# mLSTM heads: Silu in one activation, and the last two heads' convolutions behind the first head's scores

## The chip, the core and the metric

One Trainium2 chip, one of its cores, one launch. The time is the device time of a launch in microseconds, which here is the time of that core. Five engines work from instruction streams of their own: PE (TensorE, matmuls), DVE (VectorE), ACT (ScalarE), POOL (GpSimd) and SP (SyncE); the last two mostly issue DMAs in this kernel.

## The reference

A decoder layer on 512 tokens of width 1024, in float32: an mLSTM branch with 4 heads and a sliding-window attention branch (SWA) with 16 query heads, 4 key heads and a window of 128 run on the same normalised input, are gated and merged, and an MLP and a gated embedding follow. The part that the change touches makes the queries and keys of the mLSTM branch:

```python
qk_ml = jax.nn.silu(causal_depthwise_conv(qk_ml, conv_qk[i]))      # 4 taps along the tokens
q_ml, k_ml = jnp.split(qk_ml, 2, axis=-1)
q_ml = q_ml.reshape(B, S, ML_HEADS, ML_DQK) * (ML_DQK ** -0.5)     # 4 heads of 128
k_ml = k_ml.reshape(B, S, ML_HEADS, ML_DQK)
...
h_ml = mlstm_chunkwise(q_ml, k_ml, v_ml..., ig, lf)                # scores, decay, num / den
y_b = swa_with_sinks(q_sw, k_sw, v_sw, sinks[i])
```

## The kernel before

A matrix product is made of three passes of a faster float format: each float32 operand is split into a high part (a cast, `split` or `load_w`, on ACT) and a low part (the residual, on DVE), and high x high, low x high and high x low are added up in PSUM. So each weight block costs ACT a cast of 128 x 1024 (`wh`) and DVE a residual (`wl`). In PSUM there are three pools of two tiles each: `psg` for projections, `psa` for scores and transposes, `pst` for the outputs of the attention and the rest. Tiles of 128 x 512 in SBUF (`acc`, `sg`, `dm` and others) come from one ring of 34. Names in the profile are those of the tiles; `qs` is a split query of the attention, `yb` its split output, `lm` a tile of logits and then weights, `ya` the parts that the mLSTM heads use.

In which order an engine gets its instructions is set by a list scheduler that takes them in the order of the code with costs of its own, and lets a later one pass an earlier one on an engine where that one would wait. So the order below isn't the order of the code. ACT evaluates functions from a table; where the next function isn't in the loaded one, an ACT_TABLE_LOAD stands ahead of it. Exponentials, Sigmoid and Silu each ask for a load where another of the three ran before; copies and casts don't.

Two stretches matter:

- The attention loop, 236 to about 325 us: 16 units (`swa_probs`, four query heads on one block of 128 tokens each), whose scores are made two units ahead of the unit at hand. Every four units `swa_out` transposes two blocks' weights and multiplies them with the values. Between the units `fill` puts projections: those of the attention's queries (`q_proj`) and seven of the eight mLSTM tiles (`qk_proj`, in the order 0, 4, 1, 5, 2, 6, 3; tiles 0 to 3 are the heads' queries, 4 to 7 their keys).
- The head stage, about 325 to 390 us: decay matrices (`ml_decay`, exponentials on ACT), the last projection, Silu, the split into parts (`qk_parts`), scores and outputs of the four heads (`ml_scores`, `ml_out`), with blocks of the attention's branch product (`branch_b`) between.

Before, `qk_proj` convolves straight from PSUM: ACT scales the tile by the last tap into `acc`, DVE adds the three shifted taps (L854), and only then is the PSUM tile free. `silu` takes a new tile `sg` for the sigmoid and multiplies on DVE (L862), with the queries' factor 128^-0.5 in the same instruction.

Of the kernel before, what the change touches and what calls it, by code (L numbers as in the profile page):

```python
# [12 lines left out]
AF = mybir.ActivationFunctionType  # L13
ALU = mybir.AluOpType
AX = mybir.AxisListType

P = 128
S = 512
# [5 lines left out]
NH = 4  # L24
# [75 lines left out]
def block_kernel(  # L100
# [32 lines left out]
    V, A, G, T = nc.vector, nc.scalar, nc.gpsimd, nc.tensor  # L133
# [18 lines left out]
    def nm(s):  # L152
        n_names[0] += 1
        return f"{s}_{n_names[0]}"


    def ps_g():
        return pp.tile([P, 512], F32, tag="g", bufs=2, name=nm("psg"))

    def ps_t():  # L160
        return pp.tile([P, 512], F32, tag="t", bufs=2, name=nm("pst"))

    def ps_a():
        return pp.tile([P, 1024], F32, tag="a", bufs=2, name=nm("psa"))
# [6 lines left out]
    def act_f(n="f"):  # L171
        return ap.tile([P, 512], F32, tag="act", bufs=NACT, name=nm(n))
# [21 lines left out]
    def r32(t):  # L194
        return t.bitcast(F32)
# [3 lines left out]
    def split(dst, src, scale=None):  # L199

        if scale is None:
            A.copy(dst[0], src)  # L202
            last_low[0] = V.tensor_sub(dst[1], src, r32(dst[0]))  # L203
        else:
            done = A.activation(dst[0], src, AF.Copy, scale=scale)
            V.scalar_tensor_tensor(dst[1], src, scale, r32(dst[0]), ALU.mult, ALU.subtract)
            return done
# [13 lines left out]
    def load_w(src, n, dims, raw=None, cast=False):  # L221

        if raw is None:
            raw = load_raw(src, n)
        parts = [wp.tile([P, 1024], F32R, tag=t, bufs=WB, name=nm(t))[:, :n] for t in ("wh", "wl")]
        if cast:
            nc.gpsimd.dma_start(out=parts[0], in_=src)
            last_low[0] = V.tensor_sub(parts[1], raw[:, :n], r32(parts[0]))
        else:
            split(parts, raw[:, :n])  # L230
        return [q.rearrange("p (k c) -> p k c", k=dims) for q in parts]

    def pairs(a, b):

        return [(a[0], b[0]), (a[0], b[1]), (a[1], b[0])]
# [19 lines left out]
    def mm_T(ps, w, acts, first=True, last=True):  # L255

        ops = []
        for k in range(len(acts)):
            ops += pairs([q[:, k, :] for q in w], acts[k])
        chain(ps, ops, first, last)  # L260
# [31 lines left out]
    def cols(src, n, name, pool=cp):  # L292
        t = pool.tile([P, n], F32, name=name)
        nc.sync.dma_start(out=t, in_=src)
        return t
# [37 lines left out]
    cw = cols(conv, KT * 4, "cw", c1)  # L333
# [127 lines left out]
    for m in range(NT):  # L461
# [7 lines left out]
        ps = ps_g()  # L469
# [7 lines left out]
    def proj_T(wd, i, bank=ps_g):  # L477
        ps = bank()
        mm_T(ps, load_w(wd[i], KT * P, KT), hT)
        return ps  # L480
# [49 lines left out]
    for i in range(2):  # L530
        ps = ps_t()
# [3 lines left out]
        for ab in range(2):  # L535
            s, o = HALF[ab], HALF[1 - ab]
# [309 lines left out]

    qk = [None] * 8

    def qk_proj(i):
        ps = proj_T(w_qkml, i)  # L850
        acc = act_f("acc")
        A.activation(acc, ps, AF.Copy, scale=cw[:, i * 4 + 3 : i * 4 + 4])
        for s in range(1, 4):
            V.scalar_tensor_tensor(  # L854
                acc[:, s:], ps[:, : S - s], cw[:, i * 4 + 3 - s : i * 4 + 4 - s], acc[:, s:], ALU.mult, ALU.add
            )
        qk[i] = acc

    def silu(i):
        sg = act_f("sg")  # L860
        A.activation(sg, qk[i], AF.Sigmoid)
        V.scalar_tensor_tensor(qk[i], qk[i], P**-0.5 if i < 4 else 1.0, sg, ALU.mult, ALU.mult)  # L862


    yb = [None] * 8
# [108 lines left out]
    def spare():  # L974

        k = turn[0] % KT
        turn[0] += 1
        return [t[:, k, :] for t in ya_parts]

    def qk_parts(h):  # L980
        for i in (h, 4 + h):
            hl = spare()
            split(hl, qk[i])
            qk[i] = hl

    hs = [[act_f("hs") for _ in range(2)] for _ in range(NH)]
# [7 lines left out]
    def ml_decay(h):  # L994
        pr = rows[h]
        dg = act_f("dg")
        V.tensor_tensor(
            dg.rearrange("p (t j) -> p t j", t=NT),
            pr.rearrange("p (t j) -> p t j", t=NT),
            tri.unsqueeze(1).broadcast_to([P, NT, P]),  # L1000
            ALU.add,
        )
        dm = [act_f("dm") for _ in range(3)]
        wT = [dm[0], dm[1][:, :384], dm[2][:, :256], dm[2][:, 256:384]]
        for s in range(NT):
            for t in range(s, NT):
                src = dg if t == s else pr
                A.activation(
                    wT[s][:, (t - s) * P : (t - s + 1) * P],
                    src[:, t * P : (t + 1) * P],  # L1010
                    AF.Exp,
                    bias=gc[:, t * NT + s, h : h + 1],
                )
        wts[h] = dm, wT

    def ml_scores(h):

        two, one = ps_a(), ps_t()
        psc = [two[:, :512], two[:, 512:896], one[:, :256], one[:, 256:]]
        q, k = qk[h], qk[4 + h]  # L1020
        for s in range(NT):
            n0 = min(s, 2) * P
            ops = pairs([t[:, s * P : (s + 1) * P] for t in k], [t[:, n0:] for t in q])
            for j, (l, r) in enumerate(ops):
                T.matmul(psc[s], l, r, start=j == 0, stop=j == 2, skip_group_check=True)
        dm, wT = wts[h]
        hl = []
        for j, n in enumerate((512, 384, 384)):
            for s in ((0,), (1,), (2, 3))[j]:
                V.tensor_mul(wT[s], psc[s][:, P:] if s == 3 else psc[s], wT[s])  # L1030
            hl.append([t[:, :n] for t in spare()])
            split(hl[j], dm[j][:, :n])
        wts[h] = hl + [[t[:, 256:] for t in hl[2]]]
# [40 lines left out]
    def branch_b(i):  # L1074
        ps = ps_g()
        mm_T(ps, load_w(w_b[i], KT * P, KT, cast=True), yb)
        t2[i] = act_f("gb")
        V.tensor_mul(t2[i], ps, gate_of(gbd, i))
# [9 lines left out]

    ml_decay(0)
    qk_proj(7)  # L1090
    silu(0)
    silu(4)
    qk_parts(0)
    ml_scores(0)
    for h in range(1, NH):
        silu(h)
        silu(4 + h)
    rds = []
    todo = list(range(KT))
    for h in range(NH):  # L1100
        for _ in range(1 if h else 2):
            branch_b(todo.pop(0))
        if h + 1 < NH:
            ml_decay(h + 1)
            qk_parts(h + 1)
        with tc.issue_after(last_mm[0].ins):
            rds.append(ml_out(h))
        if h + 1 < NH:
            if h == 2:
                branch_b(todo.pop(0))  # L1110
            with tc.issue_after(last_mm[0].ins):
                ml_scores(h + 1)
        if h == 1:
            ml_norm([0, 1], rds)
        elif h > 1:
            ml_norm([h], rds[h:])
# [703 lines left out]
    def one(n):  # L1820
        return tp.tile([P, 1], F32, tag=n, bufs=4, name=nm(n))
# [49 lines left out]
    for m in range(NT):  # L1871
        for o, n in ((0, 512),) if m == 0 else ((0, 256), (256, 256)):
            ps = ps_g()[:, :n]
# [4 lines left out]
            if o == 0:  # L1878
                s = one("fse")
# [115 lines left out]
```

## Time and profile before

| | |
|---|---|
| runs | 863.28, 864.51, 865.06 us; median 864.51 |
| the profiled execution's own time | 864.57 us |
| its span in the profile | 862.7 us |
| granted clock of PE | 0.998 |
| busy: PE, weight load, DVE, ACT, POOL | 851.6, 741.1, 724.1, 530.4, 61.2 us |
| DMA | 125.7 MB, mean 146 GB/s |

The page's times are those of one execution. Busy time of an engine is the union of its instructions; a matmul's end is modelled, so the pace of PE is better read from the starts of its matmuls. A bracket behind a row of the timeline is the idle time of that engine ahead of the row and the instruction that ended it. A group's row gives its count, its busy time and the mean of one, then the idle time ahead of the group.

### The profile page before, as it was taken

The page shows a single profiled execution, that of the slowest core. Times are in us where ns is not written, and L with a number is a line of the kernel's source. Part 1 is how long each engine was busy: PE and PEld are TensorE (multiplying, and loading weights), DVE is VectorE, ACT ScalarE, POOL GpSimd, SP SyncE. Part 2 cuts the span into 40 slices and gives each one's busy share as a digit, 9 for nine tenths or more (in the row PEclk, how much of TensorE's full clock was granted, in tenths as well). Part 3 has the DMA queues.
Part 4 walks back from the last instruction along what each step waited for, and adds up shares of the span by engine and source line. Part 5 has one row for each costly group of instructions (what it writes and reads, how often), then busy time and mean ns, then how long its engine had stood idle before and what let it go on. Part 6 is the DMA issues. An engine that isn't in the chain of part 4 may idle for free.

```text
span 862.7 us, 12945 instructions
## 1 busy us (share of the span) xinstructions
PE 851.6 (99%) x4926; PEld 741.1 (86%) x4926; DVE 724.1 (84%) x1059; ACT 530.4 (61%) x913; POOL 61.2 (7%) x93
## 2 busy tenths in 40 slices
PE   9999999999999999999999999999999999999996
PEld 7888789999878777888888888899889989988886
DVE  7898879777788888867897799879988997899656
ACT  6776657555587667864343586458638744774743
POOL 3121111000000000000020000000000000010000
PEclk9999999999999999999999999999999999999999
DMA  8677235444411246565324381744365364634402
GB/s 289 204 179 295 89 144 189 155 147 146 148 49 50 98 147 226 202 252 200 122 39 133 98 234 38 221 129 137 75 193 147 104 174 133 172 104 131 138 1 97
DMA packets 37967, 125.70 MB, mean 146 GB/s; under 512 B 5261, under 2 KB 5261, under 8 KB 37906
## 3 DMA queue, kind: packets, MB, share of 16 engines
q1 hardware_dynamic: 28578, 95.77, 32.6%
q0 software_dynamic: 9184, 28.85, 13.9%
q8 instruction: 38, 0.62, 0.3%
q10 hardware_dynamic: 144, 0.26, 0.1%
q14 instruction: 23, 0.19, 0.1%
HBM read 106.51 MB, written 11.54 MB: 137 GB/s over the span
## 4 chain that ended last, share of the span: by engine, by line
PE 86%; issue 5%; DVE 4%; ACT 2%; DMA 2%; SPq 0%; POOL 0%; POOLq 0%; DVEq 0%; ACTq 0%
PE psp L1382 27%; PE psg L241 24%; PE psa L241 11%; PE psg L1382 9%; PE psp L241 6%; PE pst L241 4%; ACT lm L900 1%; DMA wr<-in_w_vsif 1%; PE psp L1213 1%; PE pst L945 1%; PE psa L875 1%; PE psa L876 1%; PE psa L911 1%; DVE wl L203 0%; DMA wh<-in_w_b 0%
## 5 line engine op out<-in xcount | busy, mean ns | idle before, releaser
L202 ACT CAST wh<-wr 128x1024 fp32r<-128x1024 f32 x90 | 94.8, 1054 | 81.1 <-PE psg L241 20.9
L203 DVE TENSOR_TENSOR wl<-wr,wh 128x1024 fp32r<-128x1024 f32 x90 | 109.5, 1220 | 35.7 <-ACT wh L202 35.3
L1382 PE MATMUL psp<-x,wh 128*128 128x256 f32 x672 | 121.3, 283 | 0.0
L1382 PE MATMUL psp<-wh,uf 128*128 128x512 f32 x336 | 106.1, 390 | 0.1
L1382 PEld LDWEIGHTS psp<-x,wh 128*128 128x128 f32 x672 | 105.0, 192 | 0.3
L1367 ACT CAST wh<-wr 128x1024 fp32r<-128x1024 f32 x59 | 60.5, 1049 | 59.7 <-DVE wr L1707 26.4
L1382 PE MATMUL psp<-x,wl 128*128 128x256 f32 x336 | 95.1, 283 | 0.0
L1370 DVE TENSOR_TENSOR wl<-wr,wh 128x1024 fp32r<-128x1024 f32 x59 | 71.2, 1219 | 10.3 <-ACT wh L1367 8.0
L1382 PEld LDWEIGHTS psp<-wh,uf 128*128 128x128 f32 x336 | 63.1, 188 | 14.3 <-issue 1.3
L1367 ACT CAST wh<-wd 128x1024 fp32r<-128x1024 f32 x45 | 47.2, 1049 | 33.0 <-PE psp L1382 27.8
L1382 PE MATMUL psp<-wl,uf 128*128 128x512 f32 x168 | 65.5, 390 | 0.0
L1382 PEld LDWEIGHTS psp<-x,wl 128*128 128x128 f32 x336 | 64.5, 192 | 0.0
L241 PE MATMUL psg<-h,wh 128*128 128x512 f32 x192 | 60.9, 395 | 0.7 <-DVE acc L854 0.7
L1370 DVE TENSOR_TENSOR wl<-wd,wh 128x1024 fp32r<-128x1024 f32 x45 | 54.7, 1218 | 3.1 <-ACT wh L1367 3.1
L241 PEld LDWEIGHTS psg<-h,wh 128*128 128x128 f32 x192 | 35.1, 188 | 7.5 <-DVE acc L854 0.9
L1400 DVE TENSOR_TENSOR uf<-F,uf 128x512 fp32r<-128x512 f32 (+3 forms) x36 | 35.0, 983 | 6.4 <-ACT uf L1399 6.4
L241 PE MATMUL psg<-yb,wh 128*128 128x512 f32 x128 | 40.0, 392 | 0.0
L241 PE MATMUL psg<-h,wl 128*128 128x512 f32 x96 | 37.7, 393 | 0.0
L1382 PEld LDWEIGHTS psp<-wl,uf 128*128 128x128 f32 x168 | 31.5, 188 | 6.7 <-DVE wl L1370 0.3
L1382 PE MATMUL psg<-wh,uf 128*128 128x512 f32 x112 | 36.5, 389 | 0.0
L1399 ACT CAST uf<-F 128x512 fp32r<-128x512 f32 (+3 forms) x36 | 30.7, 857 | 7.6 <-DVE F L1417 7.1
L241 PE MATMUL psg<-ya,wh 128*128 128x512 f32 x112 | 34.9, 391 | 0.0
(409 smaller groups left out, 2221.6 us busy)
## 6 DMA issues: line engine op xcount, KB each, us to landing
wr<-in_w_down SPq DMA_DIRECT2D x16, 512.0 KB, 4.6
wd<-in_w_down SPq DMA_DIRECT2D x16, 512.0 KB, 4.4
wr<-in_w_upb SPq DMA_DIRECT2D x12, 512.0 KB, 4.2
wd<-in_w_upb SPq DMA_DIRECT2D x12, 512.0 KB, 4.5
gd<-gr POOLq DMA_DIRECT2D x8, 512.0 KB, 2.9
wr<-in_w_qkml SPq DMA_DIRECT2D x8, 512.0 KB, 3.4
wr<-in_w_b SPq DMA_DIRECT2D x8, 512.0 KB, 3.4
wh<-in_w_b POOLq DMA_DIRECT2D x8, 512.0 KB, 4.6
```

The lines of the kernel that those rows point to most:

```text
L202: A.copy(dst[0], src)
L203: last_low[0] = V.tensor_sub(dst[1], src, r32(dst[0]))
L241: last_mm[0] = T.matmul(ps, l, r, start=first and i == 0, stop=last and i == len(ops) - 1, skip_group_check=parts)
L875: T.matmul(o, q[:, n * P : (n + 1) * P], kk[kp][ab][:, k0 : k0 + 256], start=True, stop=False)
L876: T.matmul(o, q[:, n * P : (n + 1) * P], kl[kp][ab][:, k0 : k0 + 256], start=False, stop=True)
L900: A.activation(lm3[:, g, :], lm3[:, g, :], AF.Exp, bias=nmx[:, g : g + 1], scale=0.125, accum_out=sm[:, g : g + 1])
L911: T.transpose(pt[:, c : c + P], pT[:, c : c + P], ident)
L1367: return [A.copy(parts[0], slots[user])]
L1370: return [V.tensor_sub(parts[1], slots[user], r32(parts[0]))]
L1382: yield T.matmul(ps, l, r, start=first and j == 0, stop=last and j == len(ops) - 1, skip_group_check=True)
L1399: h = sca(n / 512 * 0.48 + 0.05, lambda: A.copy(dst()[0], src()), deps)
L1400: return vec(n / 512 * 0.54 + 0.06, lambda: V.tensor_sub(dst()[1], src(), r32(dst()[0])), [h])
```

## The change

The convolution becomes a function of its own. Tiles of heads 0 and 1 are convolved from PSUM as before; those of heads 2 and 3 are copied from PSUM by ACT, and convolved from the copy behind the first head's scores. Sigmoid and product become one Silu in place, and the queries' factor goes into the scale of the split. The Silus of heads 0 and 1 are written ahead of the first scores, those of heads 2 and 3 behind the first head's outputs.

```diff
--- before.py
+++ after.py
@@ -846,20 +846,25 @@
 
     qk = [None] * 8
 
+    def convolve(i, src):
+        acc = act_f("acc")
+        A.activation(acc, src, AF.Copy, scale=cw[:, i * 4 + 3 : i * 4 + 4])
+        for s in range(1, 4):
+            V.scalar_tensor_tensor(
+                acc[:, s:], src[:, : S - s], cw[:, i * 4 + 3 - s : i * 4 + 4 - s], acc[:, s:], ALU.mult, ALU.add
+            )
+        qk[i] = acc
+
     def qk_proj(i):
         ps = proj_T(w_qkml, i)
-        acc = act_f("acc")
-        A.activation(acc, ps, AF.Copy, scale=cw[:, i * 4 + 3 : i * 4 + 4])
-        for s in range(1, 4):
-            V.scalar_tensor_tensor(
-                acc[:, s:], ps[:, : S - s], cw[:, i * 4 + 3 - s : i * 4 + 4 - s], acc[:, s:], ALU.mult, ALU.add
-            )
-        qk[i] = acc
+        if i % 4 < 2:
+            convolve(i, ps)
+        else:
+            qk[i] = act_f("qk")
+            A.copy(qk[i], ps)
 
     def silu(i):
-        sg = act_f("sg")
-        A.activation(sg, qk[i], AF.Sigmoid)
-        V.scalar_tensor_tensor(qk[i], qk[i], P**-0.5 if i < 4 else 1.0, sg, ALU.mult, ALU.mult)
+        A.activation(qk[i], qk[i], AF.Silu)
 
 
     yb = [None] * 8
@@ -980,7 +985,7 @@
     def qk_parts(h):
         for i in (h, 4 + h):
             hl = spare()
-            split(hl, qk[i])
+            split(hl, qk[i], P**-0.5 if i < 4 else None)
             qk[i] = hl
 
     hs = [[act_f("hs") for _ in range(2)] for _ in range(NH)]
@@ -1088,13 +1093,12 @@
 
     ml_decay(0)
     qk_proj(7)
-    silu(0)
-    silu(4)
+    for i in (0, 4, 1, 5):
+        silu(i)
     qk_parts(0)
     ml_scores(0)
-    for h in range(1, NH):
-        silu(h)
-        silu(4 + h)
+    for i in (2, 6, 3, 7):
+        convolve(i, qk[i])
     rds = []
     todo = list(range(KT))
     for h in range(NH):
@@ -1110,6 +1114,9 @@
                 branch_b(todo.pop(0))
             with tc.issue_after(last_mm[0].ins):
                 ml_scores(h + 1)
+        if h == 0:
+            for i in (2, 6, 3, 7):
+                silu(i)
         if h == 1:
             ml_norm([0, 1], rds)
         elif h > 1:
```

Where the change puts the activations: the first place is ACT in the attention loop, around 246 us, behind the copy of unit 5's logits (`lm_441`). In the kernel before, the exponentials of unit 3 (`lm_415`) follow:

```order
L888 COPY lm_441_2695<-psa_448_2715 128x512
L900 ACTIVATE lm_415_2565,sm_432_2640<-lm_415_2565,nmx_429_2634 128x128 x2
L897 ACTIVATE es_431_2638<-ds_430_2636 128x4
L900 ACTIVATE lm_415_2565,sm_432_2640<-lm_415_2565,nmx_429_2634 128x128 x2
L553 CAST qs_439_2683<-psg_434_2649 64x512
L912 COPY lm_400_2510<-psa_455_2743 128x1024
```

In the changed kernel (its line numbers are five higher here):

```order
L893 COPY lm_441_2695<-psa_448_2715 128x512
L867 ACT_TABLE_LOAD
L867 ACTIVATE acc_426_2616<-acc_426_2616 128x512
L902 ACT_TABLE_LOAD
L902 ACTIVATE es_431_2638<-ds_430_2636 128x4
L905 ACTIVATE lm_415_2565,sm_432_2640<-lm_415_2565,nmx_429_2634 128x128 x4
L553 CAST qs_439_2683<-psg_434_2649 64x512
L902 ACTIVATE es_445_2704<-ds_444_2702 128x4
```

The Silu of tile 0 (`acc_426`) has come up to here, with a table load ahead of it and another one ahead of the exponentials; three more Silus stand in the loop like this, and ACT has 24 table loads in the program, against 14.

The second place is PE some 20 us later: scores of unit 8 (`psa_495`, four pairs that need the queries 391, 438, 472 and 486), then a projection (`psg_503`) and the scores of unit 9 (`psa_508`). Before, the four pairs of unit 8 stand together, and the projection follows whole:

```order
L875 MATMUL psa_495_2928<-kk_98_541,qs_438_2680 128x256
L876 MATMUL psa_495_2928<-kl_100_543,qs_438_2680 128x256
L875 MATMUL psa_495_2928<-kk_98_541,qs_472_2828 128x256
L876 MATMUL psa_495_2928<-kl_100_543,qs_472_2828 128x256
L875 MATMUL psa_495_2928<-kk_98_541,qs_486_2894 128x256
L876 MATMUL psa_495_2928<-kl_100_543,qs_486_2894 128x256
L241 MATMUL psg_503_2956<-h_31_197,wh_505_2959 128x512
L241 MATMUL psg_503_2956<-h_32_198,wh_505_2959 128x512
L241 MATMUL psg_503_2956<-h_31_197,wl_506_2960 128x512
```

Now unit 9's first pairs and the projection's first matmuls have come between the third pair and the fourth:

```order
L880 MATMUL psa_495_2928<-kk_98_541,qs_472_2828 128x256
L881 MATMUL psa_495_2928<-kl_100_543,qs_472_2828 128x256
L880 MATMUL psa_508_2992<-kk_99_542,qs_392_2417 128x256
L881 MATMUL psa_508_2992<-kl_101_544,qs_392_2417 128x256
L880 MATMUL psa_508_2992<-kk_99_542,qs_439_2683 128x256
L881 MATMUL psa_508_2992<-kl_101_544,qs_439_2683 128x256
L241 MATMUL psg_503_2956<-h_31_197,wh_505_2959 128x512
L241 MATMUL psg_503_2956<-h_32_198,wh_505_2959 128x512
L241 MATMUL psg_503_2956<-h_31_197,wl_506_2960 128x512
L880 MATMUL psa_495_2928<-kk_98_541,qs_486_2894 128x256
L881 MATMUL psa_495_2928<-kl_100_543,qs_486_2894 128x256
```

The number of matmuls ahead of the third pair is the same in both.

The third place is what feeds PE there, DVE. Before, the residuals of the queries (`qs`, which free the projections' PSUM tiles 468 and 482) stand right behind the last residual of the attention's outputs (`yb`):

```order
L203 TENSOR_TENSOR yb_467_2786<-pst_459_2770,yb_466_2785 128x128
L203 TENSOR_TENSOR yb_467_2786<-pst_458_2765,yb_466_2785 128x128
L554 TENSOR_TENSOR qs_472_2828<-psg_468_2797,qs_472_2828 64x512
L554 TENSOR_TENSOR qs_473_2831<-psg_468_2797,qs_473_2831 64x512
L901 TENSOR_TENSOR sm_480_2854<-sm_480_2854,es_479_2852 128x4
L903 RECIPROCAL rc_481_2860<-sm_480_2854 128x4
L554 TENSOR_TENSOR qs_486_2894<-psg_482_2863,qs_486_2894 64x512
```

Now the residual of a weight block (`wl_557`) and a mask copy (L894) stand ahead of the second of them:

```order
L203 TENSOR_TENSOR yb_467_2786<-pst_459_2770,yb_466_2785 128x128
L908 RECIPROCAL rc_481_2860<-sm_480_2854 128x4
L909 TENSOR_TENSOR lm_475_2843<-lm_475_2843,rc_481_2860 128x512
L203 TENSOR_TENSOR yb_467_2786<-pst_458_2765,yb_466_2785 128x128
L203 TENSOR_TENSOR wl_557_3231<-wr_555_3228,wh_556_3230 128x1024
L554 TENSOR_TENSOR qs_472_2828<-psg_468_2797,qs_472_2828 64x512
L894 COPY_PREDICATED lm_475_2843<-later_key_92,psa_488_2900 128x512
L554 TENSOR_TENSOR qs_473_2831<-psg_468_2797,qs_473_2831 64x512
L554 TENSOR_TENSOR qs_486_2894<-psg_482_2863,qs_486_2894 64x512
```

On ACT the cast of that weight block (`wh_556`) has likewise moved from behind the third of these queries to ahead of the last output cast. The fourth place is DVE where unit 14's logits (`lm_580`) are reduced. Before, the residual ahead of it is `wl_642`, the reduction of unit 14 follows two rows later:

```order
L889 COPY_PREDICATED lm_580_3354<-later_key_92,psa_579_3345 128x512
L228 TENSOR_TENSOR wl_642_3643<-wr_640_3640,wh_641_3642 128x1024
L901 TENSOR_TENSOR sm_564_3282<-sm_564_3282,es_563_3280 128x4
L891 TENSOR_REDUCE mx_581_3357<-lm_580_3354 128x4
L903 RECIPROCAL rc_565_3288<-sm_564_3282 128x4
L893 SCALAR_TENSOR_TENSOR nmx_582_3359<-mx_581_3357,nsink_2494 128x4
```

Now it is `wl_644`, a load later of the branch's weights, and the normalisation of unit 13 and the mask's product (L923) have gone ahead of it:

```order
L906 TENSOR_TENSOR sm_564_3279<-sm_564_3279,es_563_3277 128x4
L908 RECIPROCAL rc_565_3285<-sm_564_3279 128x4
L909 TENSOR_TENSOR lm_547_3207<-lm_547_3207,rc_565_3285 128x512
L923 SCALAR_TENSOR_TENSOR pT_568_3308<-tri_97,psa_567_3298 128x1024
L894 COPY_PREDICATED lm_580_3351<-later_key_92,psa_579_3342 128x512
L228 TENSOR_TENSOR wl_644_3666<-wr_642_3663,wh_643_3665 128x1024
L896 TENSOR_REDUCE mx_581_3354<-lm_580_3351 128x4
L898 SCALAR_TENSOR_TENSOR nmx_582_3356<-mx_581_3354,nsink_2494 128x4
```

## The prediction

> **What bounds the kernel now.** I read the busy shares first, then the chain that ended last, then the busy time by stretches, and last the waits of TensorE (PE) in the stage that the change touches.
>
> ```profile
> PE 851.6 (99%) x4926; PEld 741.1 (86%) x4926; DVE 724.1 (84%) x1059; ACT 530.4 (61%) x913; POOL 61.2 (7%) x93
> ...
> PEclk9999999999999999999999999999999999999999
> ...
> PE 86%; issue 5%; DVE 4%; ACT 2%; DMA 2%; SPq 0%; POOL 0%; POOLq 0%; DVEq 0%; ACTq 0%
> ```
>
> PE is busy for 99% of the span at the full granted clock, and 86% of the chain is PE's. So a change that leaves PE's matmuls as they are can only move the time through PE's gaps: it wins those that it closes and loses those that it opens. The stretches of the stage show how much room the feeding engines have:
>
> ```profile
> core 0: us, PE busy (x) PEld busy (x) DVE busy (x) ACT busy (x) POOL busy (x), PEclk, DMA share, GB/s
> 240.00:260.00 20.00, 18.95 (x100) 14.00 (x99) 18.65 (x42) 16.54 (x54) 0.00 (x0) 1.00 0.19 55
> ...
> 340.00:360.00 20.00, 19.79 (x123) 17.63 (x122) 15.36 (x34) 15.43 (x45) 1.06 (x2) 1.00 0.67 237
> ```
>
> Columns: length, then the busy time of each engine. In 240 to 260 us VectorE (DVE) has 1.35 us free and ScalarE (ACT) 3.46; here are also PE's only early gaps. Its waits over 236 to 400 us:
>
> ```profile
> PE pst L945 <- DVE pT L918: 0.7, 1, 0.7
> PE psg L241 <- DVE acc L854: 0.7, 1, 0.7
> PE psa L875 <- DVE lm L889: 0.2, 1, 0.2
> PE psa L1025 <- DVE hd L1049: 0.2, 1, 0.2
> PE psa L911 <- DVE nmx L893: 0.2, 1, 0.2
> ...
> 250.88 0.63 PE L911 MATMUL psa<-ident,lm 128*128 128x128 f32 x4 [0.15 <-DVE nmx L893]
> ...
> 323.98 1.08 PE L945 MATMUL pst<-pT,vs 128*64 128x512 f32 x4 [0.69 <-DVE pT L918]
> ```
>
> That is 2.0 us in all, each wait for DVE; two of them stand below with their place in the timeline. This is the whole of what the change can win in this stage, a little more if measured from start to start (below).
>
> **The change part by part.** The rows that price it, ACT and then DVE, grouped over 236 to 345 us (busy, mean ns of one, idle before):
>
> ```profile
> L900 ACT ACTIVATE lm<-lm,nmx 128x128 f32<-128x128 f32 x64 | 25.0, 392 | 10.9 <-DVE nmx L893 10.7
> L888 ACT COPY lm<-psa 128x512 f32<-128x512 f32 x11 | 6.4, 584 | 0.3 <-PE psa L876 0.2
> L852 ACT ACTIVATE acc<-psg,cw 128x512 f32<-128x512 f32 x8 | 5.4, 678 | 1.6 <-PE psg L241 1.6
> L861 ACT ACTIVATE sg<-acc 128x512 f32<-128x512 f32 x8 | 5.0, 659 | 0.0
> L861 ACT ACT_TABLE_LOAD x1 | 1.3, 1283 | 0.0
> ...
> L203 DVE TENSOR_TENSOR wl<-wr,wh 128x1024 fp32r<-128x1024 f32 x7 | 8.5, 1212 | 0.0
> L854 DVE SCALAR_TENSOR_TENSOR acc<-psg,cw,acc 128x511 f32<-128x511 f32 x8 | 5.9, 741 | 0.3 <-ACT acc L852 0.3
> L862 DVE SCALAR_TENSOR_TENSOR acc<-acc,sg 128x512 f32<-128x512 f32 x8 | 5.2, 681 | 0.0
> L554 DVE TENSOR_TENSOR qs<-psg,qs 64x512 fp32r<-64x512 f32 x6 | 4.1, 688 | 1.1 <-ACT qs L553 0.8
> ```
>
> - Removed: eight products on DVE, 8 x 0.681 = 5.4 us. They stood where PE had only the 0.7 us wait for pT, so most of this was hidden work.
> - Added: four copies of PSUM to a tile on ACT, 4 x 0.584 = 2.3 us. They free PSUM earlier for the tiles of heads 2 and 3, but the one PE wait for the convolution (psg L241 <- acc L854) belongs to tile 0, which is convolved as before. Gain: nothing.
> - Moved: four convolutions go from the attention loop to behind the first head's scores, 4 x 3 x 0.741 = 8.9 us of DVE and 4 x 0.678 = 2.7 us of ACT. DVE has 4.64 us free in 340 to 360 and the product work is gone there, so the cover is the matmuls of the head stage; if it runs short, the next split or decay product comes late to PE. I take 0.3 us, with 0 and 1.5 as ends (a third of the surplus of 8.9 over 4.64).
> - The factor of q goes into the split: the scaled forms cost at most 678 against 662 and 741 against 681 by the nearest rows, four tiles, 0.3 us of hidden work.
> - Silu itself has no row. By Sigmoid (659) and the scaled copy (678) of the same shape its 8 take what the 8 Sigmoids took; if it took two of them, 5.3 us more would lie on ACT, some 0.66 at each site below.
>
> **What really moves is where the activation runs.** Sigmoid wrote a new tile and all eight stood together, behind one table load. The in-place Silu needs no tile, and in the changed order of ACT four of them stand singly inside the attention loop, each with a load ahead of it and one for the exponentials behind it: ten more loads in the program, eight in the loop, 10 x 1.283 = 12.8 us of ACT. Where a load falls now shows its price:
>
> ```profile
> 245.79 0.59 ACT L888 COPY lm<-psa 128x512 f32<-128x512 f32 x1
> 246.41 0.40 ACT L900 ACTIVATE lm<-lm,nmx 128x128 f32<-128x128 f32 x1
> ...
> 257.58 0.27 ACT L202 CAST yb<-pst 128x128 fp32r<-128x128 f32 x1 [1.02 <-PE pst L945]
> ...
> 260.81 0.42 ACT L202 CAST yb<-pst 128x128 fp32r<-128x128 f32 x2
> ...
> 305.79 0.27 ACT L202 CAST yb<-pst 128x128 fp32r<-128x128 f32 x1 [1.49 <-PE pst L945]
> ...
> 309.01 0.47 ACT L202 CAST yb<-pst 128x128 fp32r<-128x128 f32 x2 [0.19 <-DVE yb L203]
> ...
> 322.88 0.69 ACT L852 ACTIVATE acc<-psg,cw 128x512 f32<-128x512 f32 x1 [1.57 <-PE psg L241]
> 323.59 1.28 ACT L861 ACT_TABLE_LOAD   x1
> 324.88 0.63 ACT L861 ACTIVATE sg<-acc 128x512 f32<-128x512 f32 x1
> ```
>
> The load at 323.59 starts 0.02 us after the activation before it and is followed 0.01 us later by the Sigmoid: it costs its own 1.28 and nothing around it. A pair with its Silu is 1.28 + 0.66 + 1.28 = 3.2 us that ACT cannot give to the exponentials.
>
> [...]
>
> **Site 1, at 246.4.** Before, unit 3's exponentials follow the copy at 245.79; now the pair stands between. The exponentials of units 3 to 5 shift 3.2 us, and the order lets PE run 15 other matmuls ahead of the block's outputs (pst). PE's pace is read here:
>
> ```profile
> 255.59 1.08 PE L945 MATMUL pst<-pT,vd 128*64 128x512 f32 x4
> ...
> 264.89 0.28 PE L875 MATMUL psa<-kk,qs 128*128 128x256 f32 x1
> ...
> 265.42 0.63 PE L241 MATMUL psg<-h,wh 128*128 128x512 f32 x2
> ...
> 270.64 0.39 PE L241 MATMUL psg<-h,wl 128*128 128x512 f32 x1
> ```
>
> The 24 matmuls from 265.42 to 270.64 start 0.228 us apart, so 15 of them are 3.4 us: the outputs start near 259.0 instead of 255.59, PE does not wait at this place, and its wait for nmx goes. The price comes one step on. ACT's eight output casts (yb) began at 257.58 and were done with at 261.2; now they begin at 257.58 + 3.4 = 261.0. Unit 6's four exponentials, which ran partly among the query casts, now stand among them, and a weight cast of 1.05 us stands ahead of the last. The same mixture of eight casts and four exponentials took from 305.79 to 309.48, 3.7 us; with the weight cast the last yb is out at 261.0 + 3.7 + 1.05 = 265.75. DVE then owes the last yb residual (a cast's time, 0.27), the wl of that weight (1.21) and the query residual qs_472 (0.69): 267.9. PE's third pair of unit 8's scores needs that tile, has the same matmuls ahead of it in both orders, and arrived at 264.89, now 0.3 earlier: 264.6. It waits 3.3. Behind it a mask copy (as long as a product, 0.7) and qs_473 (0.69) take DVE to 269.3, which frees the PSUM tile of psg_503; PE, with six score matmuls left (four take 0.53 from 264.89 to 265.42, so 0.8), stands there at 268.7 and waits 0.6 more. Sum 3.9 if every cast of this chain is as late as I say, 2.9 if the 1.02 that ACT was idle ahead of the first cast is made up. I take 3.5; the ends are 0 (the first rival) and 6.4, the pair (3.2) on top of the 3.2 by which ACT is late already.
>
> **Sites 2 and 3**, the pairs around tiles 4 and 1: ACT had idle time there and the projection is fed from copies; what is late next is the first transposes of a block, at about PE's arrival. 0.2 us, ends 0 and 1.3 (a load exposed).
>
> **Site 4**, the pair ahead of units 12 and 13. The rows are DVE's and POOL's of before:
>
> ```profile
> 305.25 0.68 DVE L891 TENSOR_REDUCE mx<-lm 128x4 f32<-128x512 f32 x1
> ...
> 309.51 0.68 DVE L904 TENSOR_TENSOR lm<-lm,rc 128x512 f32<-128x512 f32 x1
> ...
> 309.42 0.54 POOL L227 DMA_DIRECT2D wh<-in_w_b  x1 [11.45 <-DVE rc L903]
> ...
> 314.03 1.23 DVE L228 TENSOR_TENSOR wl<-wr,wh 128x1024 fp32r<-128x1024 f32 x1 [0.39 <-DMA wh<-in_w_b]
> ```
>
> The branch's weights are loaded by POOL when PE has used up a buffer, and a residual on DVE (L228) waits for them: 4.6 us from issue to use for the second load, which gets the buffer of psg_587. Before, only the first load's residual stood ahead of unit 14's reduction, and the second behind unit 15's; in the new order the second stands right ahead of unit 14's. From the end of psg_587's chain it is 0.1 to the issue, 4.6 for the load, 1.2 for the residual, and 4.9 from reduction to normalised weights (305.25 to 310.19): 10.8 us. PE has 28 projection matmuls, 6 outputs, 8 scores and 8 transposes before unit 14's transposes, 34 x 0.228 + 16 x 0.13 = 9.8. It waits 1.0; the pair itself has delayed units 12 and 13, and what of that reaches this chain comes on top. Between 0 (the load is covered) and 3.2 (the pair whole) I take 1.2.
>
> **The sum.** Opened: 3.5 + 0.2 + 1.2 + 0.3 = 5.2 us. Closed: the waits for nmx, pT and hd, 0.2 + 0.7 + 0.2 in the table; from start to start, where the next matmul could have come 0.228 after the last, they are 0.3, 0.8 and 0.4, so 1.5. The waits for lm and acc stand ahead of the first pair and stay. Net +3.7 us. The profiled execution took 864.57 (span 862.7 and 1.87 around it), 0.06 above the median of 864.51: 868.3 against the one, 868.2 against the other.
>
> **The rivals.**
> 1. Hidden: ACT is idle for 39% of the span and the scores run two units ahead, so the pairs fit in ACT's gaps and PE sees none. For it: 10.7 us of idle before exponentials (the L900 row), which are waits for DVE that a later start can overlap. Against: the late casts meet DVE when it has 1.35 us to spare in 20, and PE's order is interleaved with DVE's step by step at 265. Time: 864.5, within 1.
> 2. Faster: with 5.4 us of products gone and 8.9 us of convolutions out of the loop, DVE, the engine in every one of the five waits, is always early. It decides from the point where the four pairs open less than 1 us together and the waits close. Against: two of the five stand before anything has left DVE. At most all 2.7 us (start to start) go: 861.8.
> 3. Every load exposed: the exponentials are on the path each time. The waits at 250.88 and 323.98 show that the softmax chain is close to PE at two places; against it, at the other two ACT works ahead. 10 x 1.283 on top: 877.4.
> [...]
>
> [...]
>
> **How the numbers follow.** Forecast (opened 4 to 7 us, so 867 to 870): 0.53. Hidden: 0.26. Faster: 0.08. Loads exposed: 0.10. Pipe emptied: 0.03. A difference under 0.2%, 1.7 us, cannot be told from none, so faster is 0.08, same 0.26 and slower 0.66. The range leaves out the faster case and most of the last two: 863.4 to 872.5; the likeliest case by itself is 867 to 870.
>
> **What would show it.** Right: eight more ACT_TABLE_LOADs between 246 and 310 us, in pairs around single Silus; a PE wait of 3 to 4 us near 265 to 270, for DVE's qs; one of 1 to 2 us ahead of unit 14's transposes near 320, behind a wl that waited for its load; ACT busier by 12.8 + 2.3 = 15 us, DVE less busy by 5.4; Silu near 660 ns. Wrong: qs cast at 261 to 265 as before (the casts were not pushed), or the four Silus back in one place, or a gap in 340 to 360 behind DVE's convolutions, which would mean that the move costs and not the loads.

## The result, and the profile after

The changed kernel takes 871.18 us (median of six runs, 868.89 to 872.27) against 864.25 us in the same runs before: 1.0078 times as long, 95% interval 1.0064 to 1.0092. The forecast was 868.2 within 863.4 to 872.5; the result lies in this range, and above the likeliest case of 867 to 870. The profiled execution is the longest of the six, 872.27 us, so its gaps show a little more than the median does.

The page's busy times, and PE's waits over 236 to 410 us (engine and line, waited for; us in all, times, longest):

```profile
PE 854.0 (98%) x4926; PEld 741.3 (85%) x4926; DVE 722.2 (83%) x1051; ACT 544.7 (63%) x927; POOL 61.3 (7%) x93
...
PE psa L880 <- DVE qs L554: 2.5, 1, 2.5
PE psa L1091 <- DVE ya L206: 1.9, 1, 1.9
PE psg L241 <- DVE acc L853: 0.7, 1, 0.7
PE psa L916 <- DVE lm L909: 0.6, 1, 0.6
PE psa L880 <- DVE lm L894: 0.5, 2, 0.3
```

ACT is 14.3 us busier and DVE 1.9 us less, with the same matmuls on PE. The old waits for nmx, pT and hd are gone; two long ones have come, for `qs` and for `ya`.

Both programs have 4926 matmuls, so the start of the n-th can be compared. How much later it starts than before:

| matmul | 1000 | 1600 | 1700 | 1800 | 1900 | 2000 | 2100 | 2300 | 2400 | 4900 |
|---|---|---|---|---|---|---|---|---|---|---|
| starts, before (us) | 174.36 | 259.36 | 277.90 | 297.55 | 316.03 | 337.80 | 353.97 | 389.95 | 410.67 | 852.04 |
| later by (us) | 0.53 | 0.23 | 4.22 | 4.23 | 4.40 | 4.69 | 5.12 | 4.43 | 7.82 | 7.76 |

Two steps make the loss: 4.0 us between matmuls 1600 and 1700, and 3.4 us between 2300 and 2400. (The first 0.5 comes ahead of anything that the change touches, and is absent or of the other sign in other traces below.)

**The first step.** ACT at the first load pair, then DVE and PE twenty us later:

```profile
246.31 0.59 ACT L893 COPY lm<-psa 128x512 f32<-128x512 f32 x1
246.92 1.28 ACT L867 ACT_TABLE_LOAD   x1
248.22 0.63 ACT L867 ACTIVATE acc<-acc 128x512 f32<-128x512 f32 x1
248.85 1.28 ACT L902 ACT_TABLE_LOAD   x1
250.15 0.21 ACT L902 ACTIVATE es<-ds 128x4 f32<-128x4 f32 x1
...
266.11 1.22 DVE L203 TENSOR_TENSOR wl<-wr,wh 128x1024 fp32r<-128x1024 f32 x1
267.36 0.69 DVE L554 TENSOR_TENSOR qs<-psg,qs 64x512 fp32r<-64x512 f32 x1
268.07 0.73 DVE L894 COPY_PREDICATED lm<-later_key,psa 128x512 f32<-128x512 int32 x1
268.84 1.41 DVE L554 TENSOR_TENSOR qs<-psg,qs 64x512 fp32r<-64x512 f32 x2
...
268.10 0.38 PE L880 MATMUL psa<-kk,qs 128*128 128x256 f32 x1 [2.49 <-DVE qs L554]
...
269.59 0.73 PE L241 MATMUL psg<-h,wh 128*128 128x512 f32 x2
```

The pair with its Silu takes 3.2 us of ACT, and each load is followed within 0.02 us of its end by the next activation. Then the chain of the forecast runs link by link: the weight residual, the first query residual, and PE's third pair of unit 8's scores the moment that one is done.

**The second step** is 130 us later. SP, DVE and PE around the last head's normalisation, then PE's clock in two stretches (columns as before; granted clock third from the end):

```profile
387.18 0.33 SPq L1176 DMA_DIRECT2D wo<-in_w_out  x1
...
393.28 1.22 DVE L1187 TENSOR_TENSOR wo<-wo,wo 128x1024 f32<-128x1024 f32 x1 [4.58 <-DMA wo<-in_w_out]
394.42 0.17 DVE L391 RECIPROCAL rs<-sd 128x4 f32<-128x4 f32 x1
...
399.14 0.66 PE L1091 MATMUL psa<-ident,hs 128*128 128x128 f32 x4 [1.88 <-DVE ya L206]
...
400.87 1.05 PE L241 MATMUL psg<-yb,wh 128*128 128x512 f32 x2
401.72 0.63 PE L241 MATMUL psg<-yb,wl 128*128 128x512 f32 x1
...
396.77:400.18 3.41, 1.53 (x10) 1.03 (x9) 3.41 (x5) 0.35 (x1) 0.00 (x0) 1.00 0.82 303
400.18:403.60 3.42, 3.42 (x10) 2.53 (x9) 1.91 (x3) 0.70 (x2) 0.00 (x0) 0.50 0.53 194
```

DVE in the kernel before:

```profile
387.23 0.18 DVE L391 RECIPROCAL rs<-sd 128x4 f32<-128x4 f32 x1 [2.96 <-ACT sd L389]
...
392.94 2.35 DVE L1180 TENSOR_TENSOR wo<-wo,wo 128x1024 f32<-128x1024 f32 x2
```

`wo` is a block of the output projection's weights; L1187 subtracts one block from another, long before anything needs the result (in the kernel before, the next row that reads a `wo` tile starts at 427.9). In the new order of DVE it stands ahead of the last head's normalisation (L391 and what follows) instead of behind it, and DVE waits 4.58 us for the load. Not all of this is loss: the normalisation needs `sd` from ACT, which was done at 391.63, and before it waited 2.96 us for that. It starts at 394.42, some 2.8 us late. So the normalised head, its transposes and their split (`ya`, L206) are late, and PE waits 2.0 us from start to start. Behind that gap PE runs at half its clock for 3.4 us (granted 0.50 from 400.18 to 403.60; two matmuls take 0.85 us from 400.87 to 401.72, 0.43 each instead of 0.228), which costs the other 1.4 us.

At gaps with 1.9 to 2.8 us of idle time the clock dropped in some executions and not in others; the last section lists them.

### The profile page after: what moved, and what is told of

It is laid out like the page before. It is cut to its first block, busy times and chain, and to the rows that moved or that the text cites. A ratio compares the mean times of both kernels' runs of the same rounds, so it can differ in the third digit from the quotient of the medians.

```text
span 870.5 us, 12951 instructions
## 1 busy us (share of the span) xinstructions
PE 854.0 (98%) x4926; PEld 741.3 (85%) x4926; DVE 722.2 (83%) x1051; ACT 544.7 (63%) x927; POOL 61.3 (7%) x93
## 4 chain that ended last, share of the span: by engine, by line
PE 88%; DVE 5%; DMA 3%; ACT 2%; issue 1%; SPq 0%; DVEq 0%; POOLq 0%; ACTq 0%
PE psp L1389 27%; PE psg L241 25%; PE psa L241 11%; PE psg L1389 9%; PE psp L241 6%; PE pst L241 4%; PE pst L950 1%; ACT lm L905 1%; DMA wr<-in_w_vsif 1%; DVE wl L203 1%; PE psp L1220 1%; DMA wo<-in_w_out 1%; DVE qs L554 1%; PE psa L880 1%; PE psa L1030 1%
```

## The experiments

The theory after the result: two losses with two causes, the load pair near 246 us and the order of `wo`. Rivals: the loads alone (the late gap follows from a late ACT), or the moved convolutions. Kernel 11 is the changed kernel itself, and every other one is a variant of one of the two. Each ratio is against runs of the kernel before on the same chip, and it is estimated from all runs, so it need not be the quotient of the medians.

| kernel | median, us (range) | ratio to before, 95% interval |
|---|---|---|
| 1: early Silus behind one load | 869.68 (866.51 to 873.41) | 1.0054 (1.0035 to 1.0073) |
| 2: wo behind the normalisation | 869.89 (868.57 to 870.26) | 1.0059 (1.0047 to 1.0071) |
| 3: both | 867.99 (866.02 to 869.36) | 1.0041 (1.0028 to 1.0054) |
| 4: Silu alone on the kernel before | 874.60 (874.11 to 875.51) | 1.0119 (1.0106 to 1.0132) |
| 5: 3, and branch residuals held | 863.97 (863.03 to 864.64) | 0.9993 (0.9984 to 1.0002) |
| 6: 5, but one pair early | 868.97 (868.63 to 869.14) | 1.0052 (1.0039 to 1.0066) |
| 7: the convolutions' move alone | 874.54 (871.39 to 875.10) | 1.0111 (1.0093 to 1.0128) |
| 8: Silu grouped, residuals held, no move | 865.36 (864.47 to 866.86) | 1.0011 (1.0002 to 1.0020) |
| 9: 5, but wo early | 865.91 (863.17 to 868.03) | 1.0010 (0.9998 to 1.0022) |
| 10: 5, and tile 0 copied too | 863.98 (862.97 to 864.49) | 0.9993 (0.9985 to 1.0002) |
| 11: the changed kernel again | 870.07 (869.26 to 871.06) | 1.0065 (1.0053 to 1.0077) |
| 12: before, residuals held | 864.05 (863.35 to 864.75) | 0.9996 (0.9986 to 1.0005) |

**1. The early Silus behind the loop's last exponential.** `issue_after` keeps the instructions made inside it behind the given one on that one's engine. In the diffs here and below, the lines that only store the instruction to wait for are left out.

```diff
-    for i in (0, 4, 1, 5):
-        silu(i)
+    with tc.issue_after(last_exp[0].ins):
+        for i in (0, 4, 1, 5):
+            silu(i)
```

> The changed kernel with the four early Silus held behind the last exponential of the attention loop, so that they share one table load; nothing else. Two-loss theory (4.0 us at unit 8's scores from the load pairs, 3.4 us near 397 us from the subtraction of the wo tiles that stands ahead of the last head's normalisation): the PE wait near 268 goes, the one near 397 stays, 871.2 - 4.0 = 867.2. Rival, all of it is the loads (the gap near 397 follows from an ACT that runs late): both gaps go, 864. Rival, the moved convolutions cost it: 871.

Measured 869.68, 2.5 over the two-loss theory. The trace, which is that of the longest of the nine runs, shows the gap near 268 gone (matmul 1700 starts when it did before, -0.05) and the late one still there (4.0 us between 2300 and 2400). New waits came, which no theory had:

```profile
PE pst L952 <- DVE pT L925: 4.2, 2, 2.8
PE psa L1093 <- DVE ya L206: 2.5, 1, 2.5
```

So the late gap does not follow from the loads in the loop.

**2. The wo subtraction behind the last normalisation.**

```diff
-            V.tensor_sub(b, b_out[3][j - 1], b)
+            with tc.issue_after(last_norm[0].ins):
+                V.tensor_sub(b, b_out[3][j - 1], b)
```

> The changed kernel with the wo subtractions held behind the last head's normalisation on DVE; the ten extra loads stay. Two-loss theory: the gap near 268 stays, the gap near 397 and the slow matmuls behind it go, 871.2 - 3.4 = 867.8. Rival, the loads make the late gap: 871. Rival, the DMA that the subtraction waits for is needed there anyway: the wait moves to the later place and 870 or more.

In the trace this is the two-loss theory as written: a step of 3.99 us between matmuls 1600 and 1700, nothing between 2300 and 2400, a span of 866.7 that is 4.0 over before. The median, 869.89, is 1.3 above the profiled execution's 868.57: within the five runs the time goes in two groups, about 868.7 and 870.1. That the late wait and the slow clock behind it hang on the order of wo is read from this trace (kernel 9 shows it from the other side); by the medians alone (871.18 and 869.89, with overlapping intervals) it would not be clear.

**3. Both edits.**

> Both edits. Two-loss theory: 871.2 - 4.0 - 3.4 = 863.8, the time of before within 1 us, with the convolutions still behind the first head's scores. Rival, the moved convolutions and copies cost something of their own: 866 or more.

Too slow for the theory by 4 us: 867.99. The two rows of pT's wait, and what stands ahead of each on DVE:

```profile
302.52 1.22 DVE L228 TENSOR_TENSOR wl<-wr,wh 128x1024 fp32r<-128x1024 f32 x1 [2.49 <-DMA wh<-in_w_b]
...
303.93 1.21 DVE L925 SCALAR_TENSOR_TENSOR pT<-tri,psa 128x1024 f32<-128x1024 f32 x1
...
305.20 1.08 PE L952 MATMUL pst<-pT,vd 128*64 128x512 f32 x4 [1.82 <-DVE pT L925]
...
323.09 1.23 DVE L228 TENSOR_TENSOR wl<-wr,wh 128x1024 fp32r<-128x1024 f32 x1 [4.83 <-issue]
324.24 2.35 DVE L925 SCALAR_TENSOR_TENSOR pT<-tri,psa 128x1024 f32<-128x1024 f32 x2
...
326.64 1.98 PE L952 MATMUL pst<-pT,vs 128*64 128x512 f32 x4 [2.28 <-DVE pT L925]
```

It is the form of the wo loss once more: a residual of the branch's weights (L228) stands on DVE ahead of work that PE needs, and DVE sits 2.5 and 4.8 us in front of it until its load is in (the second idle time is put down to "issue"; that it is the load is inferred from the first row, where a residual of the same line waits for its load; in the traces of before and of the changed kernel such a `wh` load landed 3.7 to 5.2 us after its issue). Behind the second gap the first four matmuls take 1.98 us instead of 1.08: the slow clock again (granted 0.50 from 327 to 329). So 866 or more, the number of the rival that blames the convolutions, was met; kernel 5 tells the two apart.

**4. The Silu alone on the kernel before**, without copies and without the move.

```diff
-        sg = act_f("sg")
-        A.activation(sg, qk[i], AF.Sigmoid)
-        V.scalar_tensor_tensor(qk[i], qk[i], P**-0.5 if i < 4 else 1.0, sg, ALU.mult, ALU.mult)
+        A.activation(qk[i], qk[i], AF.Silu)
...
-            split(hl, qk[i])
+            split(hl, qk[i], P**-0.5 if i < 4 else None)
```

> The kernel before with the in-place Silu and the factor in the split alone; no convolution is moved and none is copied. In its order the single Silus and their loads stand in the loop as in the changed kernel, and wo stands behind the normalisation as before. Two-loss theory: the gap near 268 alone, 864.3 + 4.0 = 868.3, a little less where the product work is missed. Rival, the convolutions' move is the cost: 864. Rival, the late gap comes from loads: 871.

874.60, the worst of all and 6.3 over the theory, which fails here. The gap near 268 is there, 2.77 us, and with it a half clock (granted 0.50 from 267 to 273) that the changed kernel's first trace doesn't have there, so that this place costs 6.0 us instead of 4.0. Five tiles' Silus stand singly in this loop, and further waits follow, which cost another 5.3 us between matmuls 1800 and 2000:

```profile
PE psa L873 <- DVE qs L554: 2.5, 1, 2.5
PE psg L241 <- DVE ds L893: 2.2, 1, 2.2
PE psg L241 <- DVE acc L854: 1.4, 2, 0.8
...
267.00:269.00 2.00, 1.89 (x7) 1.63 (x8) 1.91 (x4) 1.16 (x2) 0.00 (x0) 0.50 0.68 233
```

The wait for acc has a second instance here: PSUM of a tile that is convolved in place. That copies and moved convolutions spare the changed kernel such waits fits, but was not tested by itself, and what causes the wait of 2.2 us is not known.

**5. Both edits, and the first three branch residuals held behind pT.** The third edit, in `branch_b`:

```diff
-        mm_T(ps, load_w(w_b[i], KT * P, KT, cast=True), yb)
+        with tc.issue_after(last_pT[i - 3].ins) if i < 3 else ExitStack():
+            w = load_w(w_b[i], KT * P, KT, cast=True)
+        mm_T(ps, w, yb)
```

> The changed kernel with the early Silus behind one load, the wo subtractions behind the last normalisation, and the first three residuals of the branch's weights (L228 before) held on DVE behind the attention's masked products pT. Theory: what was left of the loss in the run with the first two edits (its waits of 1.8 and 2.3 us for pT, each behind a residual that waited for its load, and the slow matmuls behind the second) is an order on DVE and goes: 863.8, between 863 and 865. Rival, the convolutions moved behind the first head's scores are what costs: 866 or more.

863.97, as the theory has it: 0.9993 of before. The longest waits of PE over 200 to 450 us (the other two are 0.2 each):

```profile
PE psg L241 <- DVE acc L853: 0.7, 1, 0.7
PE psa L1033 <- DVE hd L1057: 0.3, 1, 0.3
```

The three edits change only the order on ACT and DVE (and, with it, the table loads: 16 instead of 24). So everything that the changed kernel loses is order. With Silu in place the moved convolutions cost next to nothing: between matmuls 2000 and 2300 this trace loses 0.5 us against before, and kernel 12, which moves none, 0.2.

**6. The same, but Silu 0 alone may run early.**

```diff
+    silu(0)
     with tc.issue_after(last_exp[0].ins):
-        for i in (0, 4, 1, 5):
+        for i in (4, 1, 5):
```

> The same kernel as the one with all three edits, but the Silu of tile 0 alone may run early; its order puts it, with a load ahead and one behind, at the place near 246 us where it stands in the changed kernel. Theory: this one pair makes the whole gap near 268, so the time is 4.0 us over the kernel with all three edits, 867.8, and up to 2 more where the clock drops behind the gap. Rival, it takes all four pairs: within 1 us of that kernel. Rival, a pair costs its own 3.2 us wherever it stands: 867.0 by a gap elsewhere.

868.97, 5.0 us over the kernel it is cut from, with the same gap at the same place:

```profile
267.58 0.38 PE L883 MATMUL psa<-kk,qs 128*128 128x256 f32 x1 [2.49 <-DVE qs L554]
```

One pair, 3.2 us of ACT, costs 4.0 us at PE (5.3 where the clock drops behind it, as in this trace: granted 0.50 from 270 to 272), and it is the whole of the first step. What the other three pairs cost is small: between matmuls 1800 and 2300 the changed kernel loses 0.8 us more than this one, and it differs there in the three pairs and in the branch residuals that are not held. No run separates these two.

**7. The move alone:** Sigmoid and product are back, copies and moved convolutions stay.

> The changed kernel with Sigmoid and product again in place of Silu, the queries' factor in the product: only the copies and the moved convolutions are left of the change. No load stands in the loop and wo follows the normalisation; the first branch residual stands ahead of unit 13's maximum and pT. Theory: one gap of some 1.9 us near 305 behind that residual, 866.1. Rival, the move is free: 864.2. Rival, the convolutions crowd the head stage: a gap in 340 to 390 and 867 or more.

874.54; the theory had 866.1 and is wrong by 8 us. The wait for pT is there as expected (1.9), but the rival of a crowded head stage has come true as well:

```profile
PE psa L1054 <- DVE ya L203: 2.4, 1, 2.4
PE pst L952 <- DVE pT L925: 1.9, 1, 1.9
PE psa L1032 <- DVE hd L1056: 1.1, 1, 1.1
...
358.17 1.23 DVE L228 TENSOR_TENSOR wl<-wr,wh 128x1024 fp32r<-128x1024 f32 x1 [3.56 <-DMA wh<-in_w_b]
```

Products and convolutions both stand in that stage on DVE, and again a residual waits 3.56 us for its load with a product and the parts `ya` behind it. How the 8 us divide between the crowding and the order was not separated. The two halves of the change, each about 10 us slower alone, are 6 to 7 slower together.

**8. Silu grouped behind one load on the kernel before, residuals held, no move.**

> The kernel before with the in-place Silu and the factor in the split, all eight Silus behind the last exponential (14 loads, as before), and the three branch residuals held behind pT; no convolution moved. Theory: DVE has 5.4 us less to do, and the wait for pT at 323.98 (0.8 us) and perhaps the one at 356.94 (0.4) go: 863.2, between 862.5 and 864.2. Rival: what DVE is spared is hidden, and the held residuals come late to the branch's first product instead: 864.5 to 866.

865.36: the rival's time, by a wait that it did not name. It is not the branch's product that waits for its residual; two waits for `hd` of 0.9 and 0.5 us came, each with a residual ahead of it on DVE that waits for its load. The first:

```profile
PE psa L1026 <- DVE hd L1050: 1.4, 2, 0.9
...
344.76 1.23 DVE L228 TENSOR_TENSOR wl<-wr,wh 128x1024 fp32r<-128x1024 f32 x1 [3.32 <-DMA wh<-in_w_b]
```

**9. Kernel 5 with wo left early.**

> The kernel with all three edits, but the wo subtraction is left where the changed kernel has it, ahead of the last head's normalisation on DVE. Theory: DVE waits some 4 us for the load of wo with the normalisation queued behind it, PE waits near 393 to 397 at the second half of the odd heads' transposes, and the slow clock behind the gap adds to it: 864.0 + 2.0 to 3.4, 866 to 867.4. Rival, without the loads ACT and the DMAs run earlier and wo has landed by then: 864.

865.91, 1.9 us over kernel 5 (and over kernel 10, which ran on the same chip), but with a spread of 4.9 us where kernel 5 has 1.6; against the kernel before the interval includes no change. In the trace, of the longest run, DVE waits as in the changed kernel and PE with it, and PE is at half its pace behind the gap (two matmuls from 395.72 to 396.57, 0.43 us each); matmuls 2300 to 2400 lose 3.8 us:

```profile
388.11 1.23 DVE L1193 TENSOR_TENSOR wo<-wo,wo 128x1024 f32<-128x1024 f32 x1 [4.45 <-DMA wo<-in_w_out]
...
393.96 0.68 PE L1096 MATMUL psa<-ident,hs 128*128 128x128 f32 x4 [2.18 <-DVE ya L206]
```

The runs reach from kernel 5's own time, 863.2, to 4 us above it. That this is the load's landing, early in some executions and late in others, fits this trace and the two of the changed kernel, but the short runs left no trace.

**10. Kernel 5 with tile 0 copied, too, and convolved from the copy.**

> The kernel with all three edits, and tile 0 too is copied from PSUM by ACT and convolved at once from the copy; the other tiles as they are. The wait of PE for PSUM at 246.4 (0.7, and 0.7 from start to start) stands behind three convolution instructions on DVE that read PSUM; a copy of 0.6 us frees the tile. Theory: 864.0 - 0.7 = 863.3. Rival, the copy and the later convolution delay the exponentials behind them on ACT and DVE, and a wait comes up at the next scores: 864 or more.

863.98, kernel 5's time: the wait for acc is gone, and one of 0.6 us for `qs` stands at 264.5 in its place, so the rival holds.

**11. The changed kernel again.**

> The changed kernel once more, on the chip of these runs, so that it and the single edits stand beside the same runs of before: 870 to 871.5. Theory: which of its executions are shorter is set by whether the clock drops behind the gaps near 268 and 397, so a trace with more slow matmuls goes with a longer time, at the same gaps.

870.07. In this trace the load of wo is in earlier, and the order is the same:

```profile
391.88 1.22 DVE L1187 TENSOR_TENSOR wo<-wo,wo 128x1024 f32<-128x1024 f32 x1 [3.01 <-DMA wo<-in_w_out]
...
397.73 0.65 PE L1091 MATMUL psa<-ident,hs 128*128 128x128 f32 x4 [0.29 <-DVE ya L206]
```

1.6 us less of wait on DVE is 1.6 less on PE, and the late step is 0.3 us instead of 3.4; but here the clock dropped behind the gap near 268, and that step is 5.3 instead of 4.0. So the two traces of one kernel come to 7.8 and 4.8 by different parts, with the first gap, 2.77 us, the same in both. The theory of the slow matmuls does not explain that difference: each trace has one stretch of half clock at these gaps, 3.41 us long in the first and about 3.4 here. What differs most is when wo landed.

**12. The kernel before, residuals held.**

> The kernel before with one edit: the first three residuals of the branch's weights held on DVE behind pT, nothing of the change. It tells what the hold is worth by itself, and so whether the change with its three repairs (864.0) is worth anything beyond it. Theory: the wait for pT at 323.98 (0.8 us from start to start) goes and the others stay, 863.5. Rival: a wait for pT is replaced by one for the held residual: 864.2.

864.05, within its interval no change. The wait for pT goes, and 0.8 us with it in the trace, but the median does not show it. Kernel 5 is worth nothing measurable over this one or over before, and no version here beats before.

## Why the prediction came out as it did

- *The loads, site 1.* Right in mechanism and place, and near in size. The forecast had the outputs at 259.0, the first cast at 261.0, the third pair at 267.9 and 3.5 us in all; less the 0.5 us by which this trace runs late from its start, they are at 259.05, 261.03 and 267.6, and the step is 4.0. The split was off: the wait at the third pair is 2.5 us by the profile, where 3.3 stood; by the starts of the matmuls 2.65 of the step lie there, and smaller waits behind it make up 1.3, where 0.6 stood. Kernel 6 against kernel 5 shows this pair alone.
- *Sites 2 and 3.* 0.2 forecast; 0.01 between matmuls 1700 and 1800.
- *Site 4.* 1.2 forecast for unit 14, where PE did not wait: the residual waited only 0.15 us for its load. Unit 15 waited 0.65 behind the next one, 0.8 from start to start, about what the wait for pT, gone now, had cost. The term was too large: the load was as good as in by then.
- *The head stage.* "I take 0.3 us, with 0 and 1.5 as ends": for the convolutions themselves that was about right (kernel 5 against kernel 12 shows 0.3). From matmul 1700 to 2300 the terms of the forecast come to 0.5 us (0.2, 1.2 and 0.3 opened, 0.8 and 0.4 closed), and the trace to 0.2.
- *The step that failed* comes behind that: the sum has no term for the end of the stage. The price of the stage was read from DVE's free time, and what came was a wait: wo's subtraction ahead of the last normalisation, 0.3 to 2.0 us, and up to 1.4 for the clock, 3.4 in the first trace. The new order showed that row; the forecast did not follow the order that far.
- *The clock* was not in the sum at all. A drop cost 1.3 us behind the first gap (kernel 11, a step of 5.3 instead of 4.0) and 1.4 behind the second (3.4, of which 2.0 is the wait). By the two traces of the changed kernel, most of the distance between 868.2 and 871.18 is this and wo. Which gap gets the drop could not be forecast from the trace of before.
- *The rivals.* "Hidden" and "faster" are out. Every load exposed (877.4) is out: of four pairs in the loop one is paid for. The chance called "pipe emptied" stands for a cost beside the load's own 1.28 us; no run shows one, and in the changed kernel's trace all eight loads of the loop are followed by the next instruction of ACT within 0.02 us of their end. Silu takes 637 ns where Sigmoid took 659 (ACT over 236 to 345 us, changed kernel):

```profile
L867 ACT ACT_TABLE_LOAD x5 | 6.4, 1283 | 1.5 <-DVE acc L853 1.3 <-DVE ds L900 0.2
L902 ACT ACT_TABLE_LOAD x4 | 5.1, 1283 | 0.0
L867 ACT ACTIVATE acc<-acc 128x512 f32<-128x512 f32 x7 | 4.5, 637 | 1.4 <-DVE acc L853 1.3
```

On DVE the instructions' own times add up to 777.7 us where they were 783.1, the 5.4 less of the forecast, and on ACT to 600.7 where they were 585.6, the 15 more. The busy time of the profile's page counts a stretch in which two instructions overlap once; by it DVE is only 1.9 us less busy and ACT 14.3 more.

## What to carry to other kernels

With Silu in place, the list scheduler put four of them singly between exponentials (five in kernel 4), and each brought a pair of loads. That it is the missing new tile that freed them is argued, not shown: no kernel here writes Silu to a new tile. If an operation needs a table of its own, look in the new order for where the loads went before counting what was saved. In the order of each engine look for every instruction that is fed by a load and ask what is queued behind it: in kernels 1, 3, 7, 8 and 9, as in the changed one, a block of weights was worked on one place too early and PE waited behind it, 0.3 to 2.8 us each time, though that work itself is 1.2 us and was needed anyway. When PE is the bound and a change only relieves engines beside it in one stretch, the best that it can win there is the sum of PE's present waits, here 2.0 us.

## What the runs showed of the hardware

- At gaps with 1.9 to 2.8 us of idle time the granted clock of PE dropped to 0.50 in some executions and not in others. In the first trace of the changed kernel it did not drop at the wait of 2.5 us near 268 and did behind the wait of 1.9 us near 399. In kernel 2 the wait of 2.5 us had no drop (its mean granted clock is 0.999), and in kernel 11 it had one. Further drops stand at the waits of 2.5 us in kernels 4 and 6, at those of 2.8 and 2.5 us in kernel 1 and at that of 2.3 us in kernel 3.
- The half clock lasted 3.41 us in the first trace of the changed kernel (400.18 to 403.60), about 3.4 in kernels 1, 3, 6 and 11, and about 6.8 in kernel 4. It cost 1.3 us in kernels 6 and 11, 1.4 in the first trace of the changed kernel and 2.0 in kernel 4. It began 0.5 us before PE's gap ended in kernel 4 (near 266.6 and 267.1) and 1.5 us after it in kernel 6 (near 269.1 and 267.58). What decides between a drop and none was not shown: the same wait went either way. Behind the gap near 268, the first trace of the changed kernel, then kernel 11 (columns as before, granted clock third from the end):

```profile
268.00:269.00 1.00, 0.64 (x3) 0.43 (x4) 0.94 (x3) 0.90 (x2) 0.00 (x0) 1.00 0.59 111
269.00:270.00 1.00, 1.00 (x6) 0.76 (x7) 0.97 (x2) 0.27 (x1) 0.00 (x0) 1.00 0.95 348
270.00:271.00 1.00, 1.00 (x7) 0.77 (x6) 0.97 (x3) 0.58 (x1) 0.00 (x0) 1.00 0.17 66
...
268.00:269.00 1.00, 0.99 (x5) 0.81 (x6) 0.97 (x2) 0.40 (x1) 0.00 (x0) 0.79 0.95 336
269.00:270.00 1.00, 1.00 (x3) 0.81 (x4) 0.97 (x2) 0.58 (x1) 0.00 (x0) 0.50 0.33 123
270.00:271.00 1.00, 1.00 (x4) 0.84 (x4) 0.26 (x2) 0.00 (x1) 0.00 (x0) 0.50 0.00 0
```

- The table loads at 246.92 and 248.85 in the changed kernel took 1.28 us of ACT each and nothing beside it: the rows around them follow one another within 0.02 us.
- Eight blocks of 512 KB for wo landed 4.0 to 6.1 us after their issue (before and the first trace of the changed kernel, 367 to 397 us). DVE's first subtraction (L1187) started 6.1 us after the issue of its block in the first trace of the changed kernel and 4.5 us in kernel 11; with the block 1.6 us earlier, PE waited 1.6 us less.
